# Adaptive max pooling: two plain load slots in place of a ring with gaps, one pooling instruction per load

## The chip, the cores and the metric

The kernel runs on one core of a Trainium2 chip. The metric is the device time in microseconds (us) of one execution; a comparison takes the median of several runs. The profile is of one execution, and its span runs from the first to the last instruction.

## The reference

The input `x` has 32 batches of 256 channels of 4096 float32 values, the output has 256 values for each channel:

```python
for i in range(output_size):                 # 256
    start = int(i * length / output_size)    # length = 4096
    end = int((i + 1) * length / output_size)
    result[:, :, i] = np.max(x[:, :, start:end], axis=-1)
```

As 4096 is 16 x 256, every output is the maximum of 16 neighbouring inputs. The input has 134.2 MB, the output 8.4 MB. Nothing is used twice, so the work is to read each input once, take maxima of 16, and write the result.

## The kernel before

The whole input is seen as one long row of windows of `W` = 16 values; there are 2,097,152 of them, 16,384 for each of the 128 partitions. All counts below are outputs per partition.

**Groups and loads.** The windows are cut into two groups, A and B. In each, partition p takes a contiguous piece of the row. A load brings a block of columns of a group into SBUF (the memory on the chip): 1024 outputs are 64 KB on each partition and 8.39 MB in all. Group A is loaded from its end to its beginning: first a small load of `FIRST` = 128 outputs (L87), then twelve of `CHUNK` = 1024 and one of 1008. Group B follows with two loads of 1024 and a last one of 912 (`last`). The sixteen large loads (L96) are numbered 0 to 15 in this document: number 12 is the one of 1008, number 15 the one of 912.

**The ring.** One tile, `ring`, holds two slots of `CHUNK + GAP` = 1024 + 152 outputs each. Loads take the slots in turn. Within a slot, a load lies either at the beginning or moved up by `GAP`, changing with each use of the slot. Each load is pooled by two VectorE instructions (`reduce_max`, L56, in the helper `pooled`): first the part of 872 outputs that the next load into this slot will overwrite, then the 152 outputs that lie outside of the next load's bytes. So the next load into the slot depends on the first of the two instructions alone, and is issued when that has ended. The first, small load lies in the gap of the first slot.

**What is kept.** The pooled results go to the tile `kept`, 15,472 outputs per partition, which holds all but the last load's results. The last load is pooled by one instruction into a free place of `ring` (`last_kept`).

**Order.** All loads are issued on SP's queue, in order, each behind the wait for its place. When all are issued, SP issues two stores out of `kept` (L117): 6712 KB of group A, then 1024 KB of group B; each waits for the poolings that it needs. The last load's 456 KB are stored from ScalarE's queue (L114) when they are pooled. VectorE does all of the computing, TensorE and ScalarE compute nothing.

Of the kernel before, what the change touches and what calls it, by code (L numbers as in the profile page):

```python
# [1 line left out]

# [4 lines left out]


@with_exitstack
def kernel(  # L10
    ctx: ExitStack,
    tc: tile.TileContext,
    x: bass.AP,
    output_size: bass.AP,
    out: bass.AP,
):

    nc = tc.nc
    P = nc.NUM_PARTITIONS
    fp32 = mybir.dt.float32

    B, C, L = x.shape
    O = int(output_size)  # L30
    assert L % O == 0, (L, O)
    W = L // O
    total = B * C * O // P
    assert B * C * O % P == 0

    CHUNK = 1024
    GAP = 152
    FIRST = 128
    LOADS_A, LOADS_B = 13, 2

    LESS = 16
    group_a = [FIRST] + [CHUNK] * (LOADS_A - 1) + [CHUNK - LESS]
    last = total - sum(group_a) - LOADS_B * CHUNK
    group_b = [CHUNK] * LOADS_B + [last]
    assert 0 < last and last * (W + 1) <= CHUNK * W

    pool = ctx.enter_context(tc.tile_pool(name="pool", bufs=1))
    ring = pool.tile([P, 2 * (CHUNK + GAP) * W], fp32, tag="ring", name="ring")
    kept = pool.tile([P, total - last], fp32, tag="kept", name="kept")

    xw = x.flatten_outer_dims().rearrange("r (o w) -> (r o) w", w=W)
    ow = out.flatten_outer_dims().rearrange("r o -> (r o)")

    def pooled(dst, at, n):

        nc.vector.reduce_max(  # L56
            out=dst,
            in_=ring[:, at * W : (at + n) * W].rearrange("p (n w) -> p n w", w=W),
            axis=mybir.AxisListType.X,
        )  # L60

    taken = 0

    def group(n):

        nonlocal taken
        span = slice(taken * P, (taken + n) * P)
        taken += n
        return (
            xw[span].rearrange("(p n) w -> p (n w)", p=P),  # L70
            ow[span].rearrange("(p n) -> p n", p=P),
        )

    stores = []
    n_loads = 0
    base = 0
    for g, loads in enumerate((group_a, group_b)):
        xg, og = group(sum(loads))
        a = sum(loads) if g == 0 else 0
        for n in loads:  # L80
            if g == 0:
                a -= n
            xn = xg[:, a * W : (a + n) * W]
            dst = kept[:, base + a : base + a + n] if n != last else None
            if n == FIRST:

                nc.sync.dma_start(  # L87
                    out=ring[:, CHUNK * W : (CHUNK + n) * W], in_=xn
                )
                pooled(dst, CHUNK, n)  # L90
            else:

                low = n_loads % 2 * (CHUNK + GAP)
                moved = n_loads // 2 % 2
                at = low + moved * GAP
                nc.sync.dma_start(out=ring[:, at * W : (at + n) * W], in_=xn)  # L96
                if n != last:
                    cut = CHUNK - GAP if moved else GAP
                    parts = [(0, cut), (cut, n)]
                    for u, v in parts if moved else parts[::-1]:  # L100
                        pooled(dst[:, u:v], at + u, v - u)
                else:
                    end = (at + CHUNK) * W
                    last_kept = ring[:, end - n : end]
                    pooled(last_kept, at, n)
                n_loads += 1
            if g:
                a += n
        full = a - last if g else sum(loads)
        stores.append((og[:, 0:full], kept[:, base : base + full]))  # L110
        base += full
    assert taken == total

    nc.scalar.dma_start(out=og[:, full : full + last], in_=last_kept)  # L114
    tc.no_sync_barrier()
    for dst, src in stores:
        nc.sync.dma_start(out=dst, in_=src)  # L117


# [1 line left out]
_INS = ['x', 'output_size']  # L121
_OUTS = [((32, 256, 256), 'float32')]

_NUMBERS = {'output_size': 256}


# [26 lines left out]
```

## Time and the profile before

| what | value |
|---|---|
| median of 3 runs (lowest to highest) | 335.14 us (334.92 to 335.22) |
| span of the profiled execution | 333.3 us |
| VectorE busy | 276.6 us, 83% of the span |
| mean DMA rate | 428 GB/s over the span |
| large loads, median from issue to landing | 24.0 us |
| the last store (456 KB), from issue to landing | 4.0 us |

The record has no separate device time for the profiled execution itself; the median of the runs stands 1.8 us above its span. In the profile, DVE is VectorE, SPq and ACTq are the queues of DMA issues of SyncE and ScalarE, and L56 is line 56 of the kernel. A group's row reads: line, engine, operation, destination <- source, their shapes, the count, then the busy time in us, the mean of one in ns, and the engine's idle time just before, with what ended it. A DMA's time to landing runs from its issue until its completion is signalled. The DMA share is the mean busy share of the core's 16 DMA engines.

### The profile page before, as it was taken

What the parts mean: (1) busy time and instruction counts of PE and PEld (TensorE: products, weight loads), DVE (VectorE), ACT (ScalarE), POOL (GpSimd) and SP (SyncE); (2) the same over time, 40 slices, a digit from 0 to 9 for tenths busy, and PEclk for the clock granted to TensorE, in tenths of its full rate; (3) what the DMA queues carried; (4) which work ended last, traced back from release to release, by engine and by line L of the source; (5) the groups of instructions that cost most, each with busy time, mean ns of one, the idle gap of its engine ahead of it and who ended that gap; (6) DMA issues with size and microseconds to landing.
All of it is one profiled execution on the core that took longest, in us unless ns stands there. A gap on an engine that the chain in (4) does not pass through costs nothing.

```text
span 333.3 us, 113 instructions
## 1 busy us (share of the span) xinstructions
DVE 276.6 (83%) x32; POOL 0.2 (0%) x4
## 2 busy tenths in 40 slices
DVE  2009979797997979799797979979797988979994
POOL 0000000000000000000000000000000000000000
DMA  9898989999898989999898989999898989899996
GB/s 377 377 503 377 503 377 488 393 425 456 377 503 377 503 377 488 393 448 433 377 503 377 503 377 488 393 456 425 389 480 381 495 377 503 377 462 448 421 412 285
DMA packets 2880, 142.61 MB, mean 428 GB/s; under 512 B 320, under 2 KB 320, under 8 KB 448
## 3 DMA queue, kind: packets, MB, share of 16 engines
q1 hardware_dynamic: 2736, 142.14, 98.7%
q10 hardware_dynamic: 144, 0.47, 0.3%
HBM read 134.22 MB, written 8.39 MB: 428 GB/s over the span
## 4 chain that ended last, share of the span: by engine, by line
DMA 57%; DVE 41%; issue 0%; SPq 0%
DMA ring<-in_x_dram 57%; DVE kept L56 36%; DVE ring L56 5%; SPq L87 0%
## 5 line engine op out<-in xcount | busy, mean ns | idle before, releaser
L56 DVE TENSOR_REDUCE kept<-ring 128x152 f32<-128x2432 f32 (+3 forms) x31 | 261.2, 8466 | 51.8 <-DMA ring<-in_x_dram 51.8
L56 DVE TENSOR_REDUCE ring<-ring 128x912 f32<-128x14592 f32 x1 | 15.4, 15353 | 0.1
L134 POOL MEMSET const-bfloat16-1.0<- 128x1 bf16 x1 | 0.1, 101 | 0.0
L134 POOL MEMSET const-uint8-127<- 128x1 uint8 x1 | 0.1, 101 | 0.0
L134 POOL MEMSET const-float32-0.0<- 128x1 f32 x1 | 0.1, 98 | 0.2 <-issue 0.2
L134 POOL MEMSET const-float32-1.0<- 128x1 f32 x1 | 0.1, 98 | 0.0
## 6 DMA issues: line engine op xcount, KB each, us to landing
ring<-in_x_dram SPq DMA_DIRECT2D x1, 8064.0 KB, 23.7
ring<-in_x_dram SPq DMA_DIRECT2D x1, 7296.0 KB, 21.9
out_dram<-kept SPq DMA_DIRECT2D x1, 6712.0 KB, 37.4
ring<-in_x_dram SPq DMA_DIRECT2D x1, 1024.0 KB, 5.0
out_dram<-kept SPq DMA_DIRECT2D x1, 1024.0 KB, 18.3
out_dram<-ring ACTq DMA_DIRECT2D x1, 456.0 KB, 4.0
ring<-in_x_dram SPq DMA_DIRECT2D x14, 24.0
```

The lines of the kernel that those rows point to most:

```text
L56: nc.vector.reduce_max(out=dst, in_=ring[:, at * W : (at + n) * W].rearrange("p (n w) -> p n w", w=W), axis=mybir.AxisListType.X,)
L134: nc = _bacc.Bacc("TRN2", target_bir_lowering=False, num_devices=1)
```

## The change

The ring with its gaps is replaced by two tiles, `slot0` and `slot1`, of 1024 outputs each. Each load takes a whole slot from its beginning, and is pooled by one instruction. The next load into that slot overwrites all of it, and waits for that one instruction. The first small load and the last load's results have tiles of their own (`first`, `last_kept`). Loads, their sizes and order, the groups, and the stores with their order are as before. SBUF use falls from 207 to 200 KB per partition.

```diff
-    ring = pool.tile([P, 2 * (CHUNK + GAP) * W], fp32, tag="ring", name="ring")
+    slots = [
+        pool.tile([P, CHUNK * W], fp32, tag=f"slot{s}", name=f"slot{s}") for s in (0, 1)
+    ]
+    first = pool.tile([P, FIRST * W], fp32, tag="first", name="first")
     kept = pool.tile([P, total - last], fp32, tag="kept", name="kept")
+    last_kept = pool.tile([P, last], fp32, tag="last_kept", name="last_kept")
...
-                low = n_loads % 2 * (CHUNK + GAP)
-                moved = n_loads // 2 % 2
-                at = low + moved * GAP
-                nc.sync.dma_start(out=ring[:, at * W : (at + n) * W], in_=xn)
-                if n != last:
-                    cut = CHUNK - GAP if moved else GAP
-                    parts = [(0, cut), (cut, n)]
-                    for u, v in parts if moved else parts[::-1]:
-                        pooled(dst[:, u:v], at + u, v - u)
-                else:
-                    end = (at + CHUNK) * W
-                    last_kept = ring[:, end - n : end]
-                    pooled(last_kept, at, n)
...
+    for k, (xg, a, n, dst) in enumerate(rows):
+        slot = slots[k % 2] if k else first
+        nc.sync.dma_start(out=slot[:, : n * W], in_=xg[:, a * W : (a + n) * W])
+        nc.vector.reduce_max(
+            out=dst,
+            in_=slot[:, : n * W].rearrange("p (n w) -> p n w", w=W),
+            axis=mybir.AxisListType.X,
+        )
```

Here `rows` lists the small load and the sixteen large ones in the order of before, `k` counts them all, and `dst` is the same place of `kept` as before, or `last_kept` for the last.

More of the change, by code (lines that the diff above doesn't have):

```diff
@@ L4 @@
 import concourse.tile as tile
-from concourse import bass_utils, mybir
+from concourse import mybir
 from concourse._compat import with_exitstack
@@ L34 @@
     assert B * C * O % P == 0
[L36 to L47, printed above, removed]
-    ring = pool.tile([P, 2 * (CHUNK + GAP) * W], fp32, tag="ring", name="ring")
-    kept = pool.tile([P, total - last], fp32, tag="kept", name="kept")
     xw = x.flatten_outer_dims().rearrange("r (o w) -> (r o) w", w=W)
     ow = out.flatten_outer_dims().rearrange("r o -> (r o)")
[L54 to L60, printed above, removed]
     taken = 0
@@ L72, in group @@
         )
[L74 to L90, printed above, removed]
-            else:
-                low = n_loads % 2 * (CHUNK + GAP)
-                moved = n_loads // 2 % 2
-                at = low + moved * GAP
-                nc.sync.dma_start(out=ring[:, at * W : (at + n) * W], in_=xn)
-                if n != last:
-                    cut = CHUNK - GAP if moved else GAP
-                    parts = [(0, cut), (cut, n)]
-                    for u, v in parts if moved else parts[::-1]:
-                        pooled(dst[:, u:v], at + u, v - u)
-                else:
-                    end = (at + CHUNK) * W
-                    last_kept = ring[:, end - n : end]
-                    pooled(last_kept, at, n)
[L106 to L111, printed above, removed]
@@ L112 @@
-    assert taken == total
-    nc.scalar.dma_start(out=og[:, full : full + last], in_=last_kept)
+    CHUNK = 1024
+    FIRST = 128
+    LESS = 16
+    loads_a = [FIRST] + [CHUNK] * 12 + [CHUNK - LESS]
+    loads_b = [CHUNK] * 2
+    last = total - sum(loads_a) - sum(loads_b)
+    assert 0 < last <= CHUNK
+    pool = ctx.enter_context(tc.tile_pool(name="pool", bufs=1))
+    slots = [
+        pool.tile([P, CHUNK * W], fp32, tag=f"slot{s}", name=f"slot{s}") for s in (0, 1)
+    ]
+    first = pool.tile([P, FIRST * W], fp32, tag="first", name="first")
@@ new lines @@
+    kept = pool.tile([P, total - last], fp32, tag="kept", name="kept")
+    last_kept = pool.tile([P, last], fp32, tag="last_kept", name="last_kept")
+    xa, oa = group(sum(loads_a))
+    xb, ob = group(sum(loads_b) + last)
+    assert taken == total
+    rows = []
+    a = sum(loads_a)
+    for n in loads_a:
+        a -= n
+        rows.append((xa, a, n, kept[:, a : a + n]))
+    for n in loads_b:
+        at = sum(loads_a) + a
+        rows.append((xb, a, n, kept[:, at : at + n]))
+        a += n
@@ L115 @@
+    rows.append((xb, a, last, last_kept[:, :]))
+    for k, (xg, a, n, dst) in enumerate(rows):
[6 more added lines that the diff above has]
+        )
+    full_b = sum(loads_b)
+    nc.scalar.dma_start(out=ob[:, full_b:], in_=last_kept[:, :])
     tc.no_sync_barrier()
-    for dst, src in stores:
-        nc.sync.dma_start(out=dst, in_=src)
+    nc.sync.dma_start(out=oa, in_=kept[:, : sum(loads_a)])
@@ L121 @@
+    nc.sync.dma_start(out=ob[:, :full_b], in_=kept[:, sum(loads_a) :])
 _INS = ['x', 'output_size']
```

## The prediction

> **What bounds the kernel now.** I read the page's slices and queues first, to see which resource is full.
>
> ```profile
> span 333.3 us, 113 instructions
> ...
> DVE 276.6 (83%) x32; POOL 0.2 (0%) x4
> ...
> q1 hardware_dynamic: 2736, 142.14, 98.7%
> q10 hardware_dynamic: 144, 0.47, 0.3%
> ```
>
> The 16 DMA engines carry packets for 98.7 + 0.3 = 99% of the span; VectorE is busy for 83%. So bytes on the DMA engines set the time, and VectorE has a little room. A table of DMA rate by stretch (columns: stretch and length in us, VectorE, GpSimd, clock, DMA share, GB/s) says how full the middle is:
>
> ```profile
> 25.08:63.79 38.71, 34.56 (x4) 0.00 (x0) 1.00 1.00 433
> 63.79:102.49 38.70, 34.56 (x4) 0.00 (x0) 1.00 1.00 434
> ```
>
> The share is 1.00: in the middle no DMA engine stands idle between two loads. Next the chain that ended last, which shows how the loads follow one another (start, length, what):
>
> ```profile
> 25.11 14.70 DVE kept L56
> 39.80 0.02 issue
> 39.82 23.98 DMA ring<-in_x_dram
> 63.79 0.02 issue
> 63.82 14.70 DVE kept L56
> ```
>
> The load that landed at 25.08 is pooled from 25.11; when its 872-output part is done (39.80), the load two further on is issued at 39.82 into mostly the same bytes and lands at 63.79. That chain has a period of 63.79 - 25.08 = 38.71 us for two loads, 19.35 us each. It looks like a bound, but 16.78 MB in 38.71 us is the 433 GB/s of the table, at DMA share 1.00: of the 23.98 us from issue to landing, the first 44.43 - 39.82 = 4.61 us are queueing behind the other load, which landed at 25.08 + 19.35 = 44.43. I call this stretch the lead: the time by which a load is issued ahead of the landing of the one before it. The lead is 4.6 us now, and the question is how much lead is needed.
>
> Last, the two instructions per load, by form (busy us, mean ns | idle before):
>
> ```profile
> L56 DVE TENSOR_REDUCE kept<-ring 128x872 f32<-128x13952 f32 x14 | 205.6, 14686 | 44.3 <-DMA ring<-in_x_dram 44.3
> L56 DVE TENSOR_REDUCE kept<-ring 128x152 f32<-128x2432 f32 x15 | 40.1, 2676 | 0.0
> ```
>
> and the start of the kernel, the only place where a load meets empty DMA engines (0 to 6 us, 40 slices of 0.15 us):
>
> ```profile
> DMA  0000000000099980168979999999999999990000
> ...
> ring<-in_x_dram SPq DMA_DIRECT2D x1, 1024.0 KB, 5.0
> ```
>
> The first load is issued at 0.73; nothing moves before 1.65 us; the slices after it are ragged, and the full rate comes at about 3 us. It lands at 5.76 (VectorE starts at 5.79 less 0.02 to 0.03 that the chain shows between landing and pooling). Its 1.049 MB at 433.5 GB/s are 2.42 us, so an unhidden load pays a start-up of 5.76 - 0.73 - 2.42 = 2.61 us, from its issue to full flow and from the last byte to the landing.
>
> **The change part by part.** *Pooling in one instruction.* From the two forms, one output costs (14686 - 2676)/720 = 16.68 ns, so 1024 outputs in one go take 14686 + 152 x 16.68 = 17221 ns, against 14686 + 2676 = 17.36 by sum, 17.28 as the timeline has the pair. VectorE saves 0.06 us a load and idles about 2.07 us per load anyway, waiting for a landing: worth nothing until the tail.
>
> *The later release.* The next load into a slot is now issued 17.22 us, not 14.70 us, after pooling begins: with the 0.02 to 0.03 us before the pooling and 0.02 behind it, 17.26 us after the landing. The other load lands 19.35 us after that landing, so the lead falls from 4.61 to 19.35 - 17.26 = 2.09 us. What is queued behind the wait on SP is only the next loads and, at the end, the two stores; no computing engine waits behind it except through the load itself. What would cover the start-up is the running load's tail, and 2.09 us of it are left.
>
> *What the start-up costs here.* No trace of before shows a load issued 2.1 us ahead. Bounds: from below, nothing is needed beyond 2.09 us and no load is late (a gain is excluded: the DMA share in the middle is 1.00 and the bytes are the same). From above, the 456 KB store at the end takes 4.0 us to land, less 1.08 us for its 0.467 MB: 2.9 us, though it runs beside the other store's tail, so this is generous. The nearest row is the first load's 2.61 us, same kind, same queue, same direction. Its issue took 0.38 us against 0.33 us for later ones, so I take 2.61 - 0.05 = 2.56, and a little less, 2.53, because engines finish a load at slightly different moments and some of the start-up overlaps. This is a choice; the range covers 2.0 to 2.9.
>
> With 2.53, a load that has a lead of 2.09 lands 0.44 us late. Being late, it gives its successor more lead: 2.09 + 0.44 = 2.53, so that one is on time. So one load of each pair is late. Number the sixteen large loads 0 to 15. Loads 0 and 1 wait for nothing. Loads 2, 4, 6, 8, 10, 12 are late by 0.44 each: 2.64 us. Load 12 is the one of 1008 outputs: it flows for 19.05 us, 0.30 less, so load 13, issued when load 11 is pooled, has 2.53 - 0.30 = 2.23 of lead and is late by 0.30. Load 14 waits for load 12's shorter pooling (16.95 us) while load 13 comes 0.30 late: lead 2.66, on time. Load 15 has 2.09 again: 0.44. Sum: 2.64 + 0.30 + 0.44 = 3.38 us.
>
> *The tail.* Here the time after the last load's landing matters:
>
> ```profile
> 276.38 17.28 DVE L56 TENSOR_REDUCE kept<-ring 128x872 f32<-128x13952 f32 x2 [2.34 <-DMA ring<-in_x_dram]
> 291.09 0.33 SPq L96 DMA_DIRECT2D ring<-in_x_dram  x1
> 291.47 21.91 SPq L117 DMA_DIRECT2D out_dram<-kept  x2
> 295.73 17.28 DVE L56 TENSOR_REDUCE kept<-ring 128x872 f32<-128x13952 f32 x2 [2.07 <-DMA ring<-in_x_dram]
> 313.06 15.35 DVE L56 TENSOR_REDUCE ring<-ring 128x912 f32<-128x14592 f32 x1
> 328.44 0.37 ACTq L114 DMA_DIRECT2D out_dram<-ring  x1
> ```
>
> The last load lands at 291.09 + 21.9 = 313.0, just when VectorE is free (295.73 + 17.28 = 313.01). From there run two covers of equal length: the pooling of 912 outputs with its store, 15.35 + 4.0 = 19.4 us, and the stores' 8.39 MB at 433 GB/s, 19.4 us. Both are unchanged and hang on the last landing, so lateness before it passes through in full; if the last load is 0.44 late, VectorE's 0.07 us saved here buys nothing. The big store is still issued about 0.4 us behind the last load and so without a gap. Separate tiles for the first load and the last result add no wait: the first load's place is used by nothing else in either kernel before it is pooled, and the last store waits for the last pooling as now.
>
> The sum is made on the profiled execution, 333.3 us of span; the three runs' median lies 1.8 us above that span, for what lies around it, which the change doesn't touch. 335.14 + 3.38 = 338.5 us.
>
> **Rule against trace.** The Trainium skill, "DMA: Bandwidth & Descriptors", section "Anatomy of one DMA", gives a transfer a fixed cost of about 2.0 us beside its bytes (measured on the GpSimd path); its section "Latency and other measured facts" has about 0.6 us to the first byte on the path that SP uses. By the 2.0 us the lead of 2.09 would suffice nearly everywhere and the sum would be an estimated +0.2 us instead of +3.4. This trace's own first load disagrees, with 0.9 us to the first flow and 2.6 us in all, but that is a cold start; hence the rival below.
>
> **The rivals.** *Hidden after all.* If what a queued load needs before its first byte passes within the running load's tail, a start-up of up to 2.09 us is covered. Only load 13, with a lead of 2.09 - 0.30 = 1.79, can be late, by 0.2 to 0.3 us: 335.3 to 335.5, no change that can be told (0.2%, 0.67 us, is about what a measurement here can tell). For it: first flow comes 0.9 us after issue, sooner than the 1.1 us left on an engine that ends the running load a microsecond ahead of its landing, and part of the 2.6 may belong to a cold start alone. Against it: the ragged 1.3 us after the first flow. It decides where start-up is below 2.1 us. The rule just named gives the same. Chance 0.15.
>
> *Partly hidden*, start-up 2.15 to 2.3 us: 7 x 0.06 to 7 x 0.21 plus 0.30, so +0.7 to +1.8. Chance 0.10.
>
> *A longer start-up on loaded engines*, up to the store's 2.9: loads 2 to 12 late by 0.81 each, loads 13, 14, 15 by 0.30, 0.24 and 0.57, together 6.0 us: 341.1. For it: the only start-up seen beside other traffic is that store's. Against it: a store's landing is written to DRAM, a load's to the chip. Chance 0.09.
>
> *Faster.* It would need VectorE on the path: 15 small instructions fewer save 15 x 0.06 = 0.9 us of VectorE's time, 334.2, if VectorE set the pace. Against it: it waits for a landing before every large load, 51.8 us in all. Chance 0.04. That one instruction would release its slot before it ends, so that nothing changed, I exclude: the trace has one release per instruction, at its end.
>
> **How the numbers follow.** The forecast, start-up 2.3 to 2.75 us (+1.8 to about +4.9), has 0.62. Slower: 0.62 + 0.10 + 0.09 = 0.81; same 0.15; faster 0.04. The range leaves out the faster case and most of the longest start-ups: 335.3 to 340.1.
>
> **What would show it.** In the profile after: one form of 1024 outputs at about 17.22 us; median from issue to landing about 21.9 us (2.53 + 19.35) instead of 24.0; landings alternating, 19.35 and 19.8 us apart; middle DMA share 0.99 instead of 1.00; the last landing at 316.4 instead of 313.0 and 19.4 us from there to the stores' end. Landings 19.35 us apart throughout would prove the hidden case; gaps over 20 us the longer one. If pooling runs longer than 17.3 us beside the loads, or the loads' own rate changes with the slots' place, the prediction is wrong in a step that I did not cost.

## The result and the profile after

The changed kernel takes 352.67 us (median of 4 runs, 352.06 to 353.42) against 335.03 us: a ratio of 1.0528 (95% interval 1.0515 to 1.0541), 17.6 us slower. The forecast was 338.5, with a range up to 340.1. The direction and the place were right, the size was off by a factor of five. Below, a run that took over 1.5% longer than the fastest of its kernel is left out of medians and ratios (one each of tail_split, gap90 and two_queues_apart).

The same lines of the page after:

```profile
span 351.3 us, 97 instructions
...
DVE 275.7 (78%) x17; POOL 0.2 (0%) x4
...
q1 hardware_dynamic: 2736, 142.14, 96.3%
q10 hardware_dynamic: 144, 0.47, 0.3%
```

VectorE has as much work as before. The DMA engines, full before, now have gaps. The same two lines tell how the 18.0 us of added span divide: packets of the loads' and stores' queue filled 0.987 x 333.3 = 329.0 us before and fill 0.963 x 351.3 = 338.3 us now. So some 9 us are packets that take longer, for the same bytes, and the other 9 us are idle engines.

The chain of waits (start, length, what) shows where:

```profile
44.19 17.23 DVE kept L77
61.42 0.02 issue
61.43 24.28 DMA slot<-in_x_dram
85.72 0.02 issue
85.74 17.23 DVE kept L77
102.97 0.02 issue
102.99 24.20 DMA slot<-in_x_dram
...
186.12 22.22 DMA slot<-in_x_dram
```

Pooling is 17.23 us instead of 14.70, as costed. But most loads take 24.2 to 24.4 us from issue to landing; 22.2, near the forecast's 21.9, comes only sometimes. The chain runs through loads 3, 5, 7 and so on, which mostly land on time, because the late load ahead of each gives it more lead. Such a load takes about as long as the late one ahead of it, plus what it is late itself. The late load 2, issued at 42.09 and landed at 66.25, is the one issue of the stretch from 41 to 48 us:

```profile
slot<-in_x_dram SPq DMA_DIRECT2D x1, 24.2
```

It queues for 2.1 us instead of 4.6, and takes 24.17 us where 2.1 + 19.35 = 21.4 would do. The period for two loads is 17.23 + 24.28 + 0.04 = 41.55 us, against 38.71.

A table by landings (stretch, length, VectorE, GpSimd, clock, DMA share, GB/s) shows the two loads of a pair:

```profile
24.81:44.16 19.35, 17.22 (x1) 0.00 (x0) 1.00 0.95 410
44.16:66.25 22.09, 17.22 (x1) 0.00 (x0) 1.00 0.97 401
66.25:85.72 19.47, 17.22 (x1) 0.00 (x0) 1.00 0.99 417
85.72:107.84 22.12, 17.22 (x1) 0.00 (x0) 1.00 0.98 409
```

The loads do mostly alternate between late and on time, but the late one is 22.09 - 19.35 = 2.74 us late, not 0.44. Read from the starts of the poolings, loads 2 to 15 are late by 2.73, 0.12, 2.78, -0.01, 2.99, -0.03, 0.78, 0.01, 2.13, 0.60, 2.67, 0.49, 0.06 and 2.98 us, 18.3 in all; the first landing happened to be 0.27 earlier than before. This is the whole difference of the spans.

How a late load begins is seen in the DMA share of 41 to 48 us, 40 slices of 0.175 us, first in the kernel after, then before (packets of 64 KB are counted in few slices, so the even rhythm of before shows as groups with zeros between; the shape counts, not the height):

```profile
DMA  9980000000000999900000999909990990000999
```

```profile
DMA  9999000000000999980000000009999800000000
```

Before, the sixteen engines move in step, a group of packet starts every 2.42 us. After, a second group stands beside the first from about 45 us on: some engines went on, others stopped. The packet records say it exactly. The load is issued at 42.09 us. The engines end their part of the running load between 43.33 and 43.81. Nine begin the new load without a pause. The other seven begin it at 44.96 to 45.88, 1.6 to 2.2 us after they ran dry and 2.9 to 3.8 us after the issue. Once begun, the load takes 20.0 to 21.1 us on each engine where 19.31 is undisturbed flow. The sixteenth completion, which is the landing, comes at 66.25. Of the 2.74 us, some 2.1 are the later beginning of the slowest engine (45.88, where the last one to go on without a pause began at 43.81), and 0.7 are its slower flow (20.03 against 19.31 us). What the flow loses is mostly in the first two packets on each engine, which take up to 3.4 us where one takes 2.42 in undisturbed flow. The spread between the first and the last engine's completion, 0.5 us at the load before, is 2.3 us at this one.

The tail is as before, shifted:

```profile
308.97 0.43 SPq L86 DMA_DIRECT2D out_dram<-kept  x1
310.76 17.22 DVE L77 TENSOR_REDUCE kept<-slot 128x1024 f32<-128x16384 f32 x1 [2.19 <-DMA slot<-in_x_dram]
328.00 0.34 SPq L87 DMA_DIRECT2D out_dram<-kept  x1
330.98 15.35 DVE L77 TENSOR_REDUCE last_kept<-slot 128x912 f32<-128x14592 f32 x1 [3.00 <-DMA slot<-in_x_dram]
346.36 0.37 ACTq L84 DMA_DIRECT2D out_dram<-last_kept  x1
```

From the last landing to the last store's landing, 346.36 + 4.1 - 330.95 = 19.5 us, as before.

### The profile page after: what moved, and what is told of

Same layout as the page of the kernel before. It is cut to its first block, busy times and chain, and to the rows that moved or that the text cites. A ratio compares the mean times of both kernels' runs of the same rounds, so it can differ in the third digit from the quotient of the medians.

```text
span 351.3 us, 97 instructions
## 1 busy us (share of the span) xinstructions
DVE 275.7 (78%) x17; POOL 0.2 (0%) x4
## 4 chain that ended last, share of the span: by engine, by line
DMA 59%; DVE 39%; SPq 0%; issue 0%
DMA slot<-in_x_dram 59%; DVE kept L77 34%; DVE last_kept L77 4%; SPq L76 0%
## 5 line engine op out<-in xcount | busy, mean ns | idle before, releaser
L77 DVE TENSOR_REDUCE kept<-slot 128x1024 f32<-128x16384 f32 (+1 forms) x15 | 258.0, 17202 | 62.1 <-DMA slot<-in_x_dram 62.1
L77 DVE TENSOR_REDUCE last_kept<-slot 128x912 f32<-128x14592 f32 x1 | 15.4, 15353 | 3.0 <-DMA slot<-in_x_dram 3.0
L77 DVE TENSOR_REDUCE kept<-first 128x128 f32<-128x2048 f32 x1 | 2.3, 2286 | 5.5 <-DMA first<-in_x_dram 5.5
## 6 DMA issues: line engine op xcount, KB each, us to landing
slot<-in_x_dram SPq DMA_DIRECT2D x1, 8064.0 KB, 24.4
slot<-in_x_dram SPq DMA_DIRECT2D x1, 7296.0 KB, 22.4
slot<-in_x_dram SPq DMA_DIRECT2D x14, 24.2
```

What stands on the lines that cost most here:

```text
L77: nc.vector.reduce_max(out=dst, in_=slot[:, : n * W].rearrange("p (n w) -> p n w", w=W), axis=mybir.AxisListType.X,)
```

## The experiments

Theory 1 was that the later issue of the loads is the whole cause; the question then was how the loss depends on the lead (the time by which a load is issued ahead of the landing of the one before it), and why it is so large.

**The ring with one instruction (ring_one).** The kernel of before, with one edit:

```diff
-                    cut = CHUNK - GAP if moved else GAP
-                    parts = [(0, cut), (cut, n)]
-                    for u, v in parts if moved else parts[::-1]:
-                        pooled(dst[:, u:v], at + u, v - u)
+                    pooled(dst, at, n)
```

> The kernel of before with its ring and gaps, but one pooling instruction per load, so that the next load into a slot waits for all of it, as after the change. Theory 1 (the later issue of the loads is the whole cause): as after the change, 351 to 354 us. Rival (the slots' places in SBUF, or the tiles of their own): 335 to 336 us, as before.

It took 352.58 us, ratio 1.0534 (1.0500 to 1.0569). The places of the slots, the tiles of their own and the store tiles do nothing that can be told; the wait for the whole slot is the change's entire effect.

**Between the two leads (gap64).** `GAP = 64` in place of 152, with the small first load in a tile `first`:

> The kernel of before with gaps of 64 outputs instead of 152 (and a tile of its own for the small first load): a load is issued about 3.16 us ahead of the landing of the one before it, between 2.09 after the change and 4.61 before. Theory 1a (a load that meets busy engines needs some 4.8 us of start-up, on its slowest engine): each pair loses 4.83 - 3.16 = 1.67 us, 7 pairs 11.7, so about 347 us. Theory 1b (only an engine that runs dry just as its new descriptors come loses time, because it stops and starts again; with 1 us more of lead none runs dry): 335 to 337 us.

345.33 us, ratio 1.0303 (1.0267 to 1.0338): 10.3 us slower than before, 1.47 a pair, so a start-up of 3.15 + 1.47 = 4.6 us on average. Theory 1b, by which another microsecond would do, fell.

**Issued later (held).** The kernel after, with a second pooling of 96 outputs of each load that a later load waits for:

```diff
+        if 0 < k < len(rows) - 2:
+            nc.vector.reduce_max(
+                out=dst[:, :96],
+                in_=slot[:, : 96 * W].rearrange("p (n w) -> p n w", w=W),
+                axis=mybir.AxisListType.X,
+            )
```

> The kernel after the change, with 96 outputs of each load pooled a second time, which holds the slot 1.75 us longer: lead 0.34 us instead of 2.09, so that most engines are idle when the next load is issued. Theory 1a (start-up 4.8 us): each pair loses 4.83 - 0.34 = 4.5 us, 7 pairs 31, about 367 us. Theory 1b (engines that are idle already start as at the kernel's beginning, 2.6 us): 2.6 - 0.34 = 2.26 us a pair, about 351 us, no slower than after the change though its loads are issued later.

355.65 us, 1.0619 (1.0604 to 1.0634). Though every slot is held 1.8 us longer, the time grows by 3.0 us alone, not by 7 x 1.75 = 12. Its chain, too, runs through the loads behind the late ones:

```profile
63.40 22.25 DMA slot<-in_x_dram
...
104.70 22.75 DMA slot<-in_x_dram
...
146.51 22.25 DMA slot<-in_x_dram
```

The late load 2 was issued at 44.04 us and landed at 66.33: issued 1.8 us later relative to the landing before it than after the change, it takes 22.29 us instead of 24.17. The six loads of this run that were issued 0.3 to 1.1 us ahead have start-ups of 2.6 to 3.4 us. Theory 1a's fixed 4.8 fell for engines that are nearly idle at the issue.

**One slot (one_slot).** `slots[0]` for all large loads, so that each meets idle engines.

> The kernel after the change with all sixteen large loads in the same slot: no load runs beside another, and each is issued to idle engines. It measures the start-up of a whole load by itself: time from issue to landing less 19.35 us of flow. If large loads have the 2.6 us of the first small one (theory 1b): 21.95 us to landing, about 632 us in all. If a large load always needs 4.8 us (theory 1a): 24.15 us to landing, about 665 us.

637.36 us (one run). The DMA issues:

```profile
slot<-in_x_dram SPq DMA_DIRECT2D x14, 22.2
```

22.2 - 19.35 = 2.85 us: this is a large load's median start-up on idle engines, a little over the 2.61 us of the small first load.

**Is it the length of the packets? (tail_split, head_split, four_dmas).** Each large load is issued as several DMAs behind the same wait. For tail_split the cuts are those below; head_split has `[0, 128, n]`, four_dmas cuts every 256 outputs.

```diff
-        nc.sync.dma_start(out=slot[:, : n * W], in_=xg[:, a * W : (a + n) * W])
+        cuts = [0, n - 128, n] if k else [0, n]
+        for u, v in zip(cuts, cuts[1:]):
+            nc.sync.dma_start(
+                out=slot[:, u * W : v * W], in_=xg[:, (a + u) * W : (a + v) * W]
+            )
```

> The kernel after the change, but each large load is issued as two DMAs, 896 outputs and then 128, behind the same wait. Each engine then ends a load with eight short packets of 8 KB (0.31 us each) instead of packets of 64 KB (2.42 us). Theory 2 (new descriptors have to reach an engine before it begins its last packet of 64 KB; about 1 us after the issue they arrive in the middle of it, and many engines stop and start again): the loss nearly goes, 336 to 340 us. Theory 1a (a load issued to busy engines needs some 4.8 us of start-up whatever the packets): 351 to 354 us.

> The kernel after the change, but each large load is issued as two DMAs, 128 outputs and then 896, behind the same wait: the short packets of 8 KB come first and every load still ends in long packets (57 KB, 2.1 us). Theory 2 (the length of the running load's last packet counts): little changes, 347 to 354 us. Rival theory 3 (the long rows of the new load are what starts slowly, and a short beginning would bridge it): 336 to 340 us. Theory 1a: 351 to 354 us.

> The kernel after the change, but each large load is issued as four DMAs of 256 outputs each behind the same wait, so that all packets have 16 KB (0.6 us). Theories 2 and 3: 336 to 341 us, as the last packet and the first are both short. Theory 1a: 351 to 354 us.

353.36 us (1.0557, 1.0514 to 1.0599), 352.77 us (1.0536, 1.0506 to 1.0567) and 351.41 us (1.0497, 1.0471 to 1.0523). None recovers anything to speak of. Neither the length of the running load's last packets nor that of the new one's first is what counts; theories 2 and 3 fell.

**Is it the queue? (two_queues, two_queues_late, two_queues_apart).** Every other load is issued by ScalarE:

```diff
+        queue = nc.scalar if k % 2 else nc.sync
-        nc.sync.dma_start(out=slot[:, : n * W], in_=xg[:, a * W : (a + n) * W])
+        queue.dma_start(out=slot[:, : n * W], in_=xg[:, a * W : (a + n) * W])
```

> The kernel after the change, with every other load issued from ScalarE's queue instead of SP's, each behind its own wait. The new load's descriptors then come in another queue than the running load's. Theory 2a (an engine that is in the last packet of a queue notices new descriptors of that same queue late): 336 to 341 us. Theories 2b (the same for the engine as a whole), 1a and 3: 350 to 354 us.

> As the run with two queues (every other load issued from ScalarE's queue), but the first load on SP's slot is held back until about 21.5 us by six extra small poolings, so that loads of the two queues don't start together and share the engines from end to end; the later ones are again issued about 2 us ahead of the landing of the one before. Theory 2a (an engine that is about to finish one queue takes up new work of that same queue late): 336 to 341 us. Theory 2b (the engine as a whole, or the loads' own start): 348 to 356 us.

> As the run before with two queues and a held-back load, but the first small load is on ScalarE's queue too, ahead of the first large one, so that it doesn't share the engines with that one. The first load on SP's queue is then issued at about 21.5 us, some 3 us ahead of the landing at 24.8, and the following loads of the two queues overlap by their lead of about 2 us only. Theory 2a (engines take up new work of the same queue late): 336 to 341 us. Theory 2b (the engine as a whole, or the loads' own start): 348 to 356 us. If the loads fall into step again, over 355 us, and the run can't tell.

359.85 us, 379.31 us and 358.18 us (1.0736, 1.1322 and 1.0631). They don't answer the question, for two queues don't take turns. In two_queues_late, the small first load on SP's queue beside the first large one on ScalarE's:

```profile
first<-in_x_dram SPq DMA_DIRECT2D x1, 1024.0 KB, 24.8
```

24.8 us for what takes 5 us alone: in this run's packet records an 8 KB packet of the short load (0.31 us) and a 64 KB packet of the long one (2.42 us) come by turns, so the short load is drawn out. The Trainium skill, "DMA: Bandwidth & Descriptors", section "Issuing engines are not separate DMA queues", says that transfers from several issuing engines run on the same 16 DMA engines and interleave; this line agrees. The next load is then issued only at 41.64 us, 16 us after the first large one has landed, and this standstill is part of the 379.31. In two_queues_apart the loads start one after the other, and yet from load 2 on the poolings come in pairs:

```profile
69.03 34.34 DVE L85 TENSOR_REDUCE kept<-slot 128x1024 f32<-128x16384 f32 x2 [7.25 <-DMA slot<-in_x_dram]
111.00 34.34 DVE L85 TENSOR_REDUCE kept<-slot 128x1024 f32<-128x16384 f32 x2 [7.63 <-DMA slot<-in_x_dram]
```

Two poolings back to back, then a wait of 7 us. The second load of the first pair lands at 85.97, just before the pooling of the first ends at 86.26, so the next load is issued at 86.28 to engines that have nothing left to do. Whether the start-up of a load beside a running one belongs to their common queue stays open.

**The rest of the curve (gap90, gap128, held_less).** `GAP = 90`, `GAP = 128`, and the second pooling of 48 outputs instead of 96.

> The kernel of before with gaps of 90 outputs: lead 3.59 us. If a load issued to busy engines needs 4.6 to 4.8 us until its slowest engine has caught up, as the runs with 2.09 and 3.16 us of lead make it: 7 x (4.7 - 3.59) = 7.8, about 343 us. If the need were the 2.9 us of a load issued to idle engines: 335 us.

> The kernel of before with gaps of 128 outputs: lead 4.22 us. By a need of 4.7 us: 7 x 0.48 = 3.4, about 338.5 us; by a need of 4.2 us or less: 335 us.

> The kernel after the change, with 48 outputs of each load pooled a second time, which holds the slot 0.95 us longer: lead 1.14 us. With 0.34 us of lead a pair lost 2.9 us, with 2.09 us 2.5 to 2.7. If the start-up depends on whether the engines are still busy at the issue, a lead between them is no better than either: 352 to 357 us. If the loss simply falls with the lead at a start-up of 2.9 us: 7 x 1.76, about 347 us; at 4.7 us: about 360 us.

341.29 us (1.0173, 1.0152 to 1.0195), 335.42 us (1.0015, 1.0006 to 1.0024) and 349.71 us (1.0446, 1.0430 to 1.0463). The last is the odd one: its slots are held 0.98 us longer than after the change, and it is 3 us faster. Its chain, again through the loads behind the late ones, and below it its one issue from 41 to 48 us, the late load 2:

```profile
44.26 17.23 DVE kept L77
61.49 0.02 issue
61.51 0.96 DVE kept L83
62.48 0.02 issue
62.49 22.45 DMA slot<-in_x_dram
...
103.20 22.20 DMA slot<-in_x_dram
```

```profile
slot<-in_x_dram SPq DMA_DIRECT2D x1, 22.4
```

The issue comes a microsecond later, and the landing comes 24.28 - 22.45 = 1.8 us sooner after it, for the late load as for the one behind it (22.4 against 24.2). With gap128 the load only queues, 4.2 + 19.35 = 23.6 us:

```profile
40.06 23.58 DMA ring<-in_x_dram
63.63 0.02 issue
63.66 15.10 DVE kept L56
```

All seven in order of the lead, which is 19.35 us less the time from a landing to the next issue into its slot as the chains have it (for gap90 by 16.68 ns an output). The loss a pair is the time over 335.0, divided by 7; the start-up is the sum of lead and loss, so it is an average that counts what both loads of a pair lose:

| kernel | lead us | time us | loss a pair us | start-up us |
|---|---|---|---|---|
| held | 0.3 | 355.7 | 3.0 | 3.3 |
| held_less | 1.1 | 349.7 | 2.1 | 3.2 |
| after the change | 2.1 | 352.7 | 2.5 | 4.6 |
| gap64 | 3.2 | 345.3 | 1.5 | 4.6 |
| gap90 | 3.6 | 341.3 | 0.9 | 4.5 |
| gap128 | 4.2 | 335.4 | 0.1 | 4.3 or less |
| before | 4.6 | 335.0 | 0 | hidden |

**Plain slots with a long lead (four_slots, three_slots).** The kernel after, with four slots and loads of 512 outputs, or three of 680; still one instruction a load, still a wait for the whole slot.

```diff
-    CHUNK = 1024
+    CHUNK = 512
...
-    loads_a = [FIRST] + [CHUNK] * 12 + [CHUNK - LESS]
-    loads_b = [CHUNK] * 2
+    loads_a = [FIRST] + [CHUNK] * 25 + [CHUNK - LESS]
+    loads_b = [CHUNK] * 5
...
-        pool.tile([P, CHUNK * W], fp32, tag=f"slot{s}", name=f"slot{s}") for s in (0, 1)
+        pool.tile([P, CHUNK * W], fp32, tag=f"slot{s}", name=f"slot{s}") for s in range(4)
...
-        slot = slots[k % 2] if k else first
+        slot = slots[k % 4] if k else first
```

> The kernel after the change with four plain slots of 512 outputs instead of two of 1024, and loads of 512: the next load into a slot still waits for all of it and one instruction pools each load, but it is issued three loads ahead, 3 x 9.68 - 8.7 = 20 us before the landing of the one before it. If the lead is the whole cause: 335 to 336 us. If whole-slot waits cost something of their own: well above that, 340 us or more.

> The kernel after the change with three plain slots and loads of 680 outputs (43.5 KB a row): lead 2 x 12.9 - 11.5 = 14 us. If only the lead counts: 335 to 335.7 us. If shorter rows flow slower, as the four slots' 9.71 us a load (19.43 for 1024 outputs against 19.35) suggests: between 335.2 and 336.6 us.

336.65 us (1.0047, 1.0034 to 1.0059) and 335.83 us (1.0024, 1.0014 to 1.0033). A whole-slot wait costs next to nothing when two or more loads are still ahead of the one that waits (leads of 20 and 14 us). The rest is the flow: in four_slots the queue's packets fill 99.0% of the span,

```profile
q1 hardware_dynamic: 5040, 142.40, 99.0%
```

and landings are 9.71 us apart, 19.43 for 1024 outputs against 19.35. Over some 15 times 1024 outputs this is 1.1 of the 1.6 us. Neither beats the kernel of before, whose DMA engines are as full with longer rows.

## Why the prediction was wrong

**What bounds the kernel, and where the change acts: right.** The DMA engines were the bound, the lead fell from 4.6 to 2.1 us, nearly every second load came late, and the lateness passed through to the end in full. ring_one shows that nothing else in the change matters.

**The pooling's price: right.** 1024 outputs take 17.219 us by the group's row, 17.221 by the sum:

```profile
L77 DVE TENSOR_REDUCE kept<-slot 128x1024 f32<-128x16384 f32 x14 | 241.1, 17219 | 57.6 <-DMA slot<-in_x_dram 57.6
```

**The start-up: this is the step that failed.** The prediction said "I take 2.61 - 0.05 = 2.56, and a little less, 2.53". In its place the runs show 4.6 us on average: a loss of 2.5 a pair, not 0.44. In the terms of the sum, loads 2, 4, 6, 8, 10 and 12 stood at 0.44 each, 2.64 together, and measured 2.73, 2.78, 2.99, 0.78, 2.13 and 2.67, 14.1 together; load 15 stood at 0.44 and measured 2.98. The value was wrong in three ways. It came from a load that meets idle engines, and even there a large load needs 2.85 (one_slot). It was then corrected downwards, for overlap with the running load; measured, that overlap costs. And its upper bound, the last store's 2.9 us, was called generous, though it was no bound for a load that meets engines about to run dry. The prediction's own two ends both came from rows in which that situation doesn't occur, and the range should have said so by reaching much further. What it left out is that some engines stop, and this is taken up next.

**Why 4.6.** In the packet records of the kernel after and of ring_one, I joined each engine's last packet of a load to its first of the next. The records don't name the engine: a packet that begins where another ends is taken for the same engine's, and engines that stopped are joined in order of time, so the counts are good to a few cases only. Engines that ran dry before the issue or up to 0.5 us after it began again mostly 1.0 to 1.3 us after the issue. Of some 40 cases that ran dry 1.25 to 1.5 us after it, half went on without a pause, and half stopped for about 1.8 us, beginning 3.2 us after the issue at the median; of some 45 cases between 1.5 and 1.75 us, about one in five stopped for about 2.0 us. From 1.75 us on stops are rare. One stopped engine of sixteen is enough to hold the landing back: at load 6 of the kernel after, fifteen engines had begun within 1.94 us of the issue, one began 3.90 us after it, and the load was 2.99 us late. The stopped engine carries its delay, so the engines drift apart: the spread of the completions, 0.6 us before, is 1 to 3 us after. While the engines are in step, a lead of 2.1 us has them run dry 1.1 to 1.7 us after the issue, in the middle of this stretch (31 of 32 at load 2 of the two traces); over all loads with that lead it is a third of them. With 1.1 us of lead they lie ahead of it (held_less: all but one of 112 before 1.1 us), with 4.2 behind it (gap128: none before 2.8 us). This is how a later issue can be faster.

So 4.6 is an average of two kinds of load. The two traces have fourteen loads with a lead of 2.0 to 2.3 us. In ten of them the slowest engine began 3.0 to 4.2 us after the issue, and the start-ups were 4.2 to 5.1 us. In two it began 1.8 and 2.2 us after it, and the start-ups were 2.7 and 2.8 us, not far from the prediction's 2.53. The other two, load 15 of each trace, don't fit: no engine began later than 1.9 us after the issue, yet their start-ups were 4.7 and 5.1 us. Their last packet on each engine took 2.9 to 4.1 us instead of 2.15; why is not shown. That engines so stop is seen in the records; what makes them stop isn't shown. It isn't the packets' length (three runs), and the queue is untested.

**The rivals.** "Hidden after all" fell: the loads with some 2.1 us of lead needed 2.7 us or more. With it fell the estimate from the Trainium skill's fixed cost of about 2.0 us ("DMA: Bandwidth & Descriptors", section "Anatomy of one DMA", measured there on the GpSimd path): the shortest start-up of a load on idle engines here is 2.35 us, that of the first small load after the change. "A longer start-up on loaded engines" was the right one, with a chance of 0.09 and a price of 6.0 us where 17.6 were measured: its 2.9 us were still too small.

**What should show it.** The prediction named gaps over 20 us between landings as the mark of the longer case, and the profile has them: 22.1. Its last landing was forecast at 316.4 and came at 330.95; the 19.4 us from there to the end measured 19.5.

## What to carry to other kernels

With two buffers, what hides a transfer's start is the time from its issue to the end of the running transfer; read it from the chain of waits. In this kernel, which is bound by DMA, 4.6 us hid it, 4.2 us was just enough and 3.6 cost 1.7%. Below that, the loss can rise when the issue comes earlier, so one more small step in the right direction may look wrong. Three plain slots of two thirds of the size give 14 us of lead, and all but 0.24% of what the ring with its gaps gave.

## What was not expected of the hardware

A load's start-up was 2.85 us on idle engines and some 4.6 us on average when it was issued 2.1 to 3.6 us ahead of the running load's landing, with single loads between 2.7 and 5.1 us at 2.1 us. The time is not monotonic in the lead: 355.7, 349.7, 352.7 and 345.3 us at 0.3, 1.1, 2.1 and 3.2 us. Two queues with every other load on each lost 6 to 7% against the kernel before (two_queues_apart, two_queues).
